# Attention values with transposed probabilities unscaled in float32 as the stationary operand, values with a column of ones moving, and scaling on the sums

## The chip, the cores and the metric

The kernel runs on one core of a Trainium2 chip. The metric is the device time of one execution in microseconds, from three runs. The profile is of one further execution, recorded by the hardware profiler.

## What is computed

The program is one layer of a decoder on 512 tokens of width 1024: a hybrid mixer, in which a recurrent branch (RG-LRU) and a sparse attention branch stand beside each other, and then a squared-ReLU MLP of width 4096. All inputs and outputs are float32. What matters here is the attention branch. Eight query heads share two groups of keys and values, and each head attends in three ways, which are gated and added:

```python
def one_block(i):
    ...
    p_c = jax.nn.softmax(sc, axis=-1) * (t >= CMP_LEN - 1)      # 31 compressed blocks
    o_c = jnp.einsum('bgrqc,bgcd->bgrqd', p_c, vc)
    ...
    p_s = jax.nn.softmax(ss.reshape(...), axis=-1)              # selected blocks
    o_s = jnp.einsum('bgrqnk,bgqnkd->bgrqd', p_s, v_sel)
    ...
    o_w = jnp.einsum('bgrqk,bgkd->bgrqd', jax.nn.softmax(sw, axis=-1), vwb)   # window
    return gb[0] * o_c + gb[1] * o_s + gb[2] * o_w
```

With 512 tokens all eight blocks are selected and the window covers all earlier tokens, so `selected` and `window` are both causal attention, over different keys and values. The attention output (512 tokens by 512) is normalised per token and multiplied with the lower half of `w_out`; the recurrent branch goes through the upper half.

## The kernel before, in words

Tokens stand in four tiles of 128. TensorE (PE) does matmuls in two ways. A float32 matrix that has been split into a high part `hi` and a rest `lo`, both of type float32r, is multiplied in three passes (`mm3`, line 986: hi·hi, hi·lo, lo·hi). Matrices that are left in plain float32 are multiplied as they are (`mm`, line 429). Splitting costs a copy (ACT or DVE) and a subtraction (DVE or POOL).

Work is written as streams, Python generators: `PR` does the projections, `AS` the attention's scores, `AV` its products with the values, `FA` the attention's end, `VW` the recurrent branch, `RS` the residual, `AD` the conditioning, `W` the loads and splits of weights, and later `TH` and `UF` (turning the normalised residual, first MLP slices), `UP`, `DA` and `DN` (MLP). They only record nodes: `Clocks.issue` and `Clocks.put` (lines 395 and 343) note each instruction with its operands and an assumed cost. `Clocks.flush` (line 237) then writes the instructions out in a list schedule: for each engine the ready node with the highest rank comes next, and the rank is the node's longest way to the end plus an offset from the table `AHEAD` (a number for every 20 steps of a stream). Where an operation may run on more than one engine (`choose`, `either`, `copy`), a letter of the table `PLACE` picks it: `a` ACT, `d` DVE, `p` POOL. So the order on every engine is fixed by these two tables and by the recorded costs, and the engines then run their instructions in that order.

Attention is cut into 16 units, each of one key group, one tile `i` of 128 queries and two heads (`UNITS`, line 46). For a unit and a head, `att_scores` (line 1416) multiplies queries and keys into a PSUM bank `s`. DVE adds the position bias and takes the row minimum `mx` on the way to a row of probabilities `p` in SBUF. ACT takes the exponential in place, one instruction for each of the three segments (compressed, selected, window), and its accumulator gives the segment's sum into `sm` (line 1464). Then `den`, the reciprocal of the sum times the gate's denominator, is made (lines 1465 to 1469), and each of the six segments is multiplied by its column of `den` in place (line 1473), on ACT, DVE or POOL.

`att_values` (line 1477) turns the scaled probabilities with PE, 128 by 128 at a time, four to a bank `tp` (line 1505), so that keys stand on partitions. It splits the bank into `hi` (copy, line 1508) and `lo` (subtraction, line 1509), both tiles `pt` from a ring of four. The values `V` and `VC` are the stationary operand, 128 wide: 64 columns of `hi` and 64 of `lo`, split once at lines 1085, 1086, 1124 and 1126. For each of the 2(i+1)+1 key blocks of a unit there are two matmuls of 256 columns (two heads by 128 queries), one with `hi` and one with `lo` (lines 1518 and 1520). All of them add into one bank `pv`. The upper 64 partitions (from the values' `lo`) are copied out by ACT into `oc` (line 1523) and added to the lower 64 by DVE (line 1525) into `att`. So `att` has features on partitions and queries along the row.

`att_finish` (line 1531) takes each finished tile of `att`: squares it (ACT), folds the squares by two additions, sums over partitions with a matmul against `ones`, and splits `att` into `hi` and `lo`, the stationary operands of the lower half of the output projection (line 1215, weights `o1..`). The upper half (weights `o0..`, line 1196) uses the recurrent branch. In the profile both halves are matmuls `f<-hi_o,h` and `f<-lo_o,h`. After them `residual` (line 1383) normalises, adds and normalises again per tile. `turn_h` (line 1567) turns the result and splits it into `h2` and `h2l`, and `up_first` (line 1596) begins the MLP with matmuls of 256 columns.

Of the kernel before, what the change touches and what calls it, by code (L numbers as in the profile page):

```python
# [32 lines left out]
RW = 528  # L33
G_LAST = 2
# [3 lines left out]
PART_BUFS = 4  # L38
SL = (0.0, 8.6, 11.4, 5.2)
# [67 lines left out]
    '': 'ad',  # L107
    'AS': 'ddd.p.a.ddapa..pdaddppapaa..paaadppd.d.pdadap.aa..ddd..pdadadd.dpa..a...a.d.adp.d.ddpa.add..paaa'
        'adpdpapaappd.aaa',
    'AV': '.ddaddd..d.dd...aadadaada..aaad..a...aaaaad.a.aaa..ada..',  # L110
    'AW': 'a.ad.aa.ddpp..dd',
    'DA': 'dd..d.dd.dddd.pa..dp..pdp.a..d...papd..dd.d.d.ddd..a.d.dap.a.d.pddpddd..pdd.d.appa.pa.pdddd.a..d'
        'pd.padp.pdd..d.ddda..a.p..adpapdddpd..pd..da.d.pddpa.dd.d.p.d..p...ddp...dd.ad.d',
    'DN': 'd..da.a.ada..d.d.pa.ad..a.ada.dd.da.ad.....dada...a....da.a...d..p.p....p.d.',
    'FA': 'd.....ppdd..',
    'RS': 'pdadddd.....',
    'TH': '..ddaa.p.a.ddad...dpadd..dpd.ad.',
    'UP': '.d.dddp..ppdd...pdp.dpp.d.ppdddd',
    'VW': '.ppdp.d.d.p..ppp.d.',
    'WS': 'a...a...a.ap.d..a.d.ap.d...p..adadapad..ddadd.apa.a.ada.ad.ad..dd.ddd.d.d.pd..d.ad.dp.dpadda.a..'  # L120
        '.d.dp...ad..a.dadda.dddad.dp.d.a..dd..a..dp.dp.d.ddd.pa.p..p.d..apda.dadddd.ddd.adddpddp..a.pddd'
        'dd.add.ddpd.dadp.d....p.d..ddadad..dd.dadpad.d..d.dda.da.....a.d.d..dd..ppada...ad..dd..a...a.a.'
        'd.ada.pda.ddpd.da..da.add......da.add.a.ad.dada.ddadddddadad.dada.',
    'XN': 'a.addd.dd.a.',
# [10 lines left out]
class Clocks:  # L135
# [370 lines left out]
    def zero(self, out):  # L506
        self.issue("pool", 0.1 + out.free_size() / 1100, [out], [], lambda: self.nc.gpsimd.memset(out, 0.0))
# [211 lines left out]
def block_kernel(tc, inp, out):  # L719
# [55 lines left out]
    def pt_tile(dt):  # L775
        return small(mp, "pt", 4, [P, 512], dt)
# [87 lines left out]
    for g in range(2):  # L864
        clk.zero(K2[g][64 - 64 * g:128 - 64 * g].bitcast(F32))
# [283 lines left out]
    def projections():  # L1149
        for g in range(2):  # L1150
            clk.zero(VC[g].bitcast(F32))
# [696 lines left out]
```

## Time and profile before

| | us |
|---|---|
| median of three runs | 644.36 (642.27 to 644.39) |
| the profiled execution | 643.96 |
| its span, from the first to the last instruction | 642.1 |
| busy: PE, DVE, ACT, POOL | 606.2, 550.3, 352.1, 179.9 |
| first and last transposes of probabilities `tp<-ident,p` | 115.5 and 268.4 |
| first and last exponentials of scores `p<-p,mx` | 101.9 and 258.3 |
| last `att<-pv,oc` | 271.7 |

A row of the profile's groups names the code line, the engine, the operation, then output and inputs by tile name, the shape, and the count after an x; behind the bar come busy time, the mean duration in ns, and the idle time of the engine in front of the group with what ended it. Busy time is the union of the records' durations. A matmul's record lasts longer than the distance to the next matmul, since matmuls are pipelined, so a PE that is busy for the whole of a stretch may still have free places in it. A row of the windows gives a stretch, its length, busy time with instruction count for PE, its weight loads (PEld), DVE, ACT and POOL, then the granted clock of PE, the share of the DMA engines and GB/s. A row of the timeline gives start, duration, engine, line, instruction and count.

### The profile page before, as it was taken

What the parts mean: (1) busy time and instruction counts of PE and PEld (TensorE: products, weight loads), DVE (VectorE), ACT (ScalarE), POOL (GpSimd) and SP (SyncE); (2) the same over time, 40 slices, a digit from 0 to 9 for tenths busy, and PEclk for the clock granted to TensorE, in tenths of its full rate; (3) what the DMA queues carried; (4) which work ended last, traced back from release to release, by engine and by line L of the source; (5) the groups of instructions that cost most, each with busy time, mean ns of one, the idle gap of its engine ahead of it and who ended that gap; (6) DMA issues with size and microseconds to landing.
All of it is one profiled execution on the core that took longest, in us unless ns stands there. A gap on an engine that the chain in (4) does not pass through costs nothing.

```text
span 642.1 us, 9070 instructions
## 1 busy us (share of the span) xinstructions
PE 606.2 (94%) x3060; PEld 499.8 (78%) x3060; DVE 550.3 (86%) x1097; ACT 352.1 (55%) x706; POOL 179.9 (28%) x175
## 2 busy tenths in 40 slices
PE   6899999997989999989999999999999999999992
PEld 6778788965776878868888878888878887888881
DVE  7988789989999999886898677575988779899988
ACT  6645436699999899786342332322332236645553
POOL 5010110424451013343212423653364212130022
PEclk9999999999999999997999999999999999999997
DMA  8968986430432202004764345343544425567613
GB/s 349 413 227 288 338 291 223 150 106 33 165 104 93 68 2 67 0 34 132 261 208 147 139 140 187 104 160 98 166 138 134 154 66 196 199 195 228 198 35 131
DMA packets 29431, 102.15 MB, mean 159 GB/s; under 512 B 3269, under 2 KB 3525, under 8 KB 29385
## 3 DMA queue, kind: packets, MB, share of 16 engines
q1 hardware_dynamic: 29240, 101.50, 46.1%
q8 instruction: 24, 0.39, 0.2%
q14 instruction: 23, 0.18, 0.1%
q10 hardware_dynamic: 144, 0.07, 0.0%
HBM read 99.47 MB, written 2.10 MB: 158 GB/s over the span
## 4 chain that ended last, share of the span: by engine, by line
PE 67%; DVE 15%; ACT 9%; DMA 6%; issue 2%; POOL 0%; DVEq 0%; ACTq 0%
PE f L434 36%; PE s L434 12%; PE pv L434 10%; PE tp L434 7%; DVE p L479 4%; ACT r L445 2%; DVE fT L479 2%; PE tp L438 2%; ACT p L445 2%; ACT h L445 2%; DVE pt L479 1%; ACT L445 1%; DMA p<-in_ada_a 1%; DVE r L479 1%; DVE h L479 1%
## 5 line engine op out<-in xcount | busy, mean ns | idle before, releaser
L434 PE MATMUL f<-h,lo_f 128*128 128x512 f32 x224 | 87.2, 389 | 0.0
L434 PE MATMUL f<-h,hi_f 128*128 128x512 f32 x224 | 87.2, 389 | 0.0
L434 PE MATMUL f<-h2l,hi_f 128*128 128x512 f32 x224 | 87.2, 389 | 0.0
L445 ACT ACTIVATE hi_f<-raw_f 128x1024 fp32r<-128x1024 f32 x25 | 26.3, 1067 | 45.2 <-PE f L434 26.4
L479 DVE TENSOR_TENSOR lo_f<-raw_f,hi_f 128x1024 fp32r<-128x1024 f32 x31 | 40.3, 1301 | 11.4 <-ACT hi_f L445 11.1
L434 PEld LDWEIGHTS f<-h,lo_f 128*128 128x128 f32 x224 | 42.1, 188 | 8.8
L434 PEld LDWEIGHTS f<-h2l,hi_f 128*128 128x128 f32 x224 | 42.1, 188 | 8.7
L434 PEld LDWEIGHTS f<-h,hi_f 128*128 128x128 f32 x224 | 42.1, 188 | 8.5
L445 ACT ACTIVATE p<-p,mx 128x32 f32<-128x32 f32 (+4 forms) x96 | 45.1, 473 | 1.8 <-DVE mx L479 1.5
L434 PE MATMUL f<-hi_o,h 128*128 128x512 f32 x128 | 44.2, 402 | 1.3 <-DVE h L479 1.3
L479 POOL TENSOR_TENSOR fT<-fT 128x512 f32<-128x512 f32 x19 | 28.3, 1492 | 54.3 <-ACT fT L445 54.3
L434 PE MATMUL pv<-pt,V 128*128 128x256 f32 x160 | 37.8, 328 | 0.9 <-ACT pt L445 0.7
L445 ACT ACTIVATE fT<-f 128x512 f32<-128x512 f32 x30 | 17.6, 588 | 37.5 <-PE f L434 37.5
L438 PE MATMUL tp<-ident,p 128*128 128x128 f32 x192 | 35.3, 274 | 0.8 <-DVE pt L479 0.7
L434 PE MATMUL s<-K,Q 128*128 128x288 f32 (+4 forms) x128 | 30.9, 332 | 5.1 <-DVE Q L479 3.4
L479 DVE TENSOR_TENSOR pt<-tp,pt 128x512 fp32r<-128x512 f32 (+1 forms) x56 | 32.9, 604 | 1.6 <-ACT pt L445 1.3
L438 PEld LDWEIGHTS tp<-ident,p 128*128 128x128 f32 x192 | 24.2, 140 | 8.3 <-DVE pt L479 2.6
L434 PEld LDWEIGHTS pv<-pt,V 128*128 128x128 f32 x160 | 26.2, 189 | 5.5 <-DVE pt L479 2.0
L445 ACT ACTIVATE fs<-fT 128x512 fp32r<-128x512 f32 x29 | 18.0, 626 | 18.8 <-PE s L434 9.7
L434 PEld LDWEIGHTS s<-K,Q 128*128 128x128 f32 x128 | 20.5, 188 | 9.9 <-DVE Q L479 3.4
L434 PEld LDWEIGHTS f<-hi_o,h 128*128 128x128 f32 x128 | 23.5, 188 | 5.6 <-DVE h L479 1.7
L434 PE MATMUL pv<-r,fs 128*128 128x512 f32 x96 | 25.8, 397 | 1.3 <-DVE r L479 1.3
(731 smaller groups left out, 1791.6 us busy)
## 6 DMA issues: line engine op xcount, KB each, us to landing
raw_f<-in_wf SPq DMA_DIRECT2D x32, 512.0 KB, 3.4
p<-in_ada_a SPq DMA_DIRECT2D x16, 512.0 KB, 8.4
ar<-in_ada_t SPq DMA_DIRECT2D x16, 512.0 KB, 5.2
ar<-in_ada_r SPq DMA_DIRECT2D x16, 512.0 KB, 4.0
r<-in_x SPq DMA_DIRECT2D x8, 512.0 KB, 5.8
raw_c<-in_wc SPq DMA_DIRECT2D x8, 512.0 KB, 4.9
raw_o<-in_wo SPq DMA_DIRECT2D x8, 512.0 KB, 3.5
raw_a<-in_wa SPq DMA_DIRECT2D x8, 384.0 KB, 7.9
```

The costliest lines, as they stand in the source:

```text
L434: lambda: self.nc.tensor.matmul(out, lhs, rhs, start=start, stop=stop))
L438: self.issue("pe", 0.109, [out], [src], lambda: self.nc.tensor.transpose(out, src, ident))
L445: return "act", cost, lambda: self.nc.scalar.activation(out, src, func, scale=scale, bias=bias, **kw), func
L479: return eng, cost, lambda: fn(out, *args, **kw), None
```

## The change

Probabilities are left unscaled. The exponential no longer writes its accumulator, `sm`, `den` and the six scalings of a unit go from `att_scores`, and `att_values` turns the unscaled probabilities. The turned block stays in float32 and is copied once. It is now the stationary operand, one block of one head at a time. The values are plain float32, 64 columns and a 65th of ones, and move. So a unit makes two matmuls of 65 columns for each key block (one for each head), and three sums for each head in one bank `pv`: three segments, two heads, 65 columns, where the 65th column holds the segment's sum of probabilities. `den` is made from these columns, one DVE multiplication scales all six blocks of 64 columns out of PSUM into `ov`, and two additions add the three segments into `att`, which now has queries on partitions. Groups of four transposes now hold up to four blocks of one head after the other, and the ring `pt` keeps its four buffers.

The values are copied once (ACT or DVE) and not split, and six fills on POOL write ones and zeros. `att_finish` squares `att` on ACT with the accumulator giving the row sum, turns `att` with four transposes, copies the bank to `hi` and subtracts for `lo`. It also waits for the event `yp` now. `AHEAD` and `PLACE` are other tables of numbers and letters, so the order and the engines of all streams change, the projections and the MLP among them.

```diff
-    'AV': [142.8, -8.6, 3.3, -42.5, -12.0, -9.0, 3.2, 261.5, 714.0, 604.8, -11.7, 349.8, 1400.4, 517.5, 179.8,
+    'AV': [507.0, -148.0, 17.4, 136.7, -64.4, 13.5, 178.9, 274.1, 572.1, 179.1, -46.5, 1110.1, 1841.6, 933.7,
...
-    V = [clk.lone(mp, [P, 4, P], F32R, name=f"V{t}") for t in range(NT)]
-    VC = [clk.lone(mp, [P, P], F32R, name=f"VC{g}") for g in range(2)]
+    V = [clk.lone(mp, [P, 4, VW_], F32, name=f"V{t}") for t in range(NT)]
+    VC = [clk.lone(mp, [P, 96], F32, name=f"VC{g}") for g in range(2)]
...
-            act(V[t][:, :, 0:64], src, AF.Copy)
-            dve("tensor_sub", V[t][:, :, 64:128], src, V[t][:, :, 0:64].bitcast(F32))
+            clk.copy(V[t][:, :, 0:64], src)
...
-                            act(seg, seg, AF.Exp, scale=-1.0, bias=col, accum_out=sm[:, si, e:e + 1])
-            den = small(mp, "den", 4, [P, 3, 2])
-            either("tensor_mul", den, sm, eg1[i][:, :, g, 2 * pair:2 * pair + 2])
-            dve("reciprocal", den, den)
...
-            for si, (a, b) in enumerate(segs):
-                for e in range(2):
-                    seg = tiles[e][:, a - base:b - base]
-                    clk.copy(seg, seg, den[:, si, e:e + 1])
+                            act(seg, seg, AF.Exp, scale=-1.0, bias=col)
...
-                    hi, lo = pt_tile(F32R)[:, :w], pt_tile(F32R)[:, :w]
-                    clk.copy(hi, tp[:, :w])
-                    dve("tensor_sub", lo, tp[:, :w], hi.bitcast(F32))
+                    pt = pt_tile(F32)[:, :w]
+                    clk.copy(pt, tp[:, :w])
...
-                        mm(po, v, hi[:, sl], done == 0, False)
-                        done += 1
-                        mm(po, v, lo[:, sl], False, done == n)
-            o = att[i][:, tok(2 * g + pair)]
-            oc = small(mp, "oc", 2, [64, 256])
-            act(oc, po[64:128, :], AF.Copy)
-            for e in range(2):
-                dve("tensor_add", o[64 * e:64 * e + 64], po[0:64, tok(e)], oc[:, tok(e)])
+                    for k, (e, _, v, si, first, last) in enumerate(sub):
+                        mm(po[:, si, e, :], pt[:, tok(k)], v, first, last)
+            den = small(mp, "den", 4, [P, 3, 2])
+            dve("tensor_mul", den, po[:, :, :, 64], eg1[i][:, :, g, 2 * pair:2 * pair + 2])
+            dve("reciprocal", den, den)
+            if i == 0:
+                dve("tensor_scalar", den[:, 0, :], den[:, 0, :], cmask, None, op0=ALU.mult)
+            ov = small(mp, "ov", 2, [P, 3, 2, 64])
+            dve("tensor_mul", ov, po[:, :, :, 0:64], den.unsqueeze(3).to_broadcast([P, 3, 2, 64]))
+            o = att[i][:, tok(2 * g + pair)].rearrange("p (e d) -> p e d", e=2)
+            either("tensor_add", ov[:, 0], ov[:, 0], ov[:, 1])
+            either("tensor_add", o, ov[:, 0], ov[:, 2])
...
-            yield after(f"pv{t}", lambda: clk.ready(att[t]))
-            sq = cmt[:, 0:512]
-            act(sq, att[t], AF.Square)
-            hi, lo = h_tile(), h_tile()
-            act(hi, att[t], AF.Copy)
-            either("tensor_sub", lo, att[t], hi.bitcast(F32))
-            for w in (256, 128):
-                either("tensor_add", sq[:, 0:w], sq[:, 0:w], sq[:, w:2 * w])
...
-            mm(ps[:, 0:1], sq[:, 0:P], ones[:, 0:1], True, True)
+            yield after(f"pv{t}", after("yp", lambda: max(clk.ready(att[t]), bank_free("tp"))))
             r = scol()
-            dve("tensor_copy", r, ps[:, 0:1])
+            act(junk[:, 0:512], att[t], AF.Square, accum_out=r)
...
+            for k in range(4):
+                turn(ps[:, tok(k)], att[t][:, tok(k)], ident)
+            hi, lo = h_tile(), h_tile()
+            clk.copy(hi, ps)
+            dve("tensor_sub", lo, ps, hi.bitcast(F32))
```

Two places show what the tables and the new steps do to the order. The first is PE where attention ends, before the change: the last products with the values of the last unit (`pv`), then a transpose for the MLP (`tp<-ident,r`) and the output projection (`f`).

```order
L434 MATMUL pv_733<-pt_738,V_122 128x256
L434 MATMUL pv_733<-pt_739,V_122 128x256
L434 MATMUL pv_733<-pt_738,V_123 128x256
L434 MATMUL pv_733<-pt_739,V_123 128x256
L434 MATMUL pv_733<-pt_743,VC_124 128x256
L434 MATMUL pv_733<-pt_744,VC_124 128x256
L438 MATMUL tp_773<-ident,r_282_502 128x128
L434 MATMUL f_745<-lo_o_662,h_650 128x512
```

The same place on PE after the change: the last products have 65 columns and one block of one head each.

```order
L439 MATMUL tp_657<-ident,p_644 128x128 x2
L435 MATMUL pv_652<-V_120,pt_656 128x65
L435 MATMUL pv_652<-V_121,pt_656 128x65
L435 MATMUL pv_652<-V_122,pt_656 128x65
L435 MATMUL pv_652<-V_123,pt_658 128x65
L435 MATMUL pv_652<-VC_124,pt_658 128x65
L435 MATMUL f_661<-hi_o_530,h_513 128x512
L435 MATMUL f_692<-hi_o_582,h_517 128x512
```

Behind the last product with the values there are 43 matmuls of the output projection before the change and 97 after it; the transposes for the MLP, which began there before, come later.

The second place is DVE in the last unit before the change: subtractions for `lo`, a scaling by `den`, the residual's rows `r`, and the two additions into `att`.

```order
L479 TENSOR_SCALAR p_704<-p_704,den_715 128x32
L479 TENSOR_TENSOR pt_736<-tp_734,pt_735 128x512
L479 SCALAR_TENSOR_TENSOR r_282_502<-f_740,stat,r_282_502 128x512
L479 CAST pt_743<-tp_742 128x256
L479 TENSOR_TENSOR pt_739<-tp_737,pt_738 128x512
L479 TENSOR_TENSOR pt_744<-tp_742,pt_743 128x256
L479 TENSOR_TENSOR r_282_502<-r_282_502,h_469 128x512
L479 TENSOR_TENSOR r_282_502<-r_282_502,h_470 128x512
L479 TENSOR_TENSOR att_129<-pv_733,oc_747 64x128 x2
```

The same place on DVE after the change: one copy of a turned bank, `den`, the scaling out of PSUM, the additions, and splits of the output projection's weights between them.

```order
L480 COPY pt_658<-tp_657 128x256
L480 TENSOR_TENSOR den_659<-pv_652,eg_133 128x6
L480 RECIPROCAL den_659<-den_659 128x6
L480 TENSOR_TENSOR ov_660<-pv_652,den_659 128x384
L480 SCALAR_TENSOR_TENSOR lo_o_694<-raw_o_532,vecs,hi_o_693 128x512
L480 TENSOR_TENSOR ov_660<-ov_660 128x128
L480 SCALAR_TENSOR_TENSOR lo_o_694<-raw_o_532,vecs,hi_o_693 128x512
L480 TENSOR_TENSOR att_129<-ov_660 128x128
L480 SCALAR_TENSOR_TENSOR r_318_547<-f_692,stat,r_318_547 128x512
L480 CAST h_666<-tp_665 128x512
L480 TENSOR_TENSOR h_667<-tp_665,h_666 128x512
```

The three subtractions and the scaling are gone from this stretch. The rows `r` of the residual, which stood between the unit's steps, come behind them.

More of the change, by code (lines that the diff above doesn't have):

```diff
@@ L33 @@
 RW = 528
+VW_ = 80
 G_LAST = 2
@@ L38 @@
 PART_BUFS = 4
+PT_BUFS = 4
 SL = (0.0, 8.6, 11.4, 5.2)
@@ L504, in copy, with fill @@
         self.choose([out], [src] + cols, "ad", *ways)
-    def zero(self, out):
-        self.issue("pool", 0.1 + out.free_size() / 1100, [out], [], lambda: self.nc.gpsimd.memset(out, 0.0))
+    def fill(self, out, value=0.0):
+        self.issue("pool", 0.1 + out.free_size() / 1100, [out], [], lambda: self.nc.gpsimd.memset(out, value))
     def dve(self, what, out, *args, **kw):
@@ L1031, in block_kernel @@
     blk = blkt.rearrange("p a b -> p (a b)")[:, :2048].rearrange("p (v l c) -> p v l c", v=2, l=16)
-    clk.zero(blkt.rearrange("p a b -> p (a b)")[:, :2048])
+    clk.fill(blkt.rearrange("p a b -> p (a b)")[:, :2048])
     cmt = clk.lone(mp, [P, 768], F32, name="cmt")
@@ L1124, in compress_out @@
             act(VC[g][0:32, 0:64], pc2[:32, 64 * g:64 * g + 64], AF.Copy)
-        for g in range(2):
-            dve("tensor_sub", VC[g][0:32, 64:128], pc2[:32, 64 * g:64 * g + 64], VC[g][0:32, 0:64].bitcast(F32))
         events.add("vc")
@@ L1150, in projections @@
         for g in range(2):
-            clk.zero(VC[g].bitcast(F32))
+            clk.fill(VC[g])
+            clk.fill(VC[g][0:32, 64:65], 1.0)
+        for t in range(NT):
+            clk.fill(V[t][:, :, 64:65], 1.0)
         load(cmt[:, 0:384], inp["w2"])
         rnn["xpad"] = r8()
-        clk.zero(rnn["xpad"][:, :, 0:3])
+        clk.fill(rnn["xpad"][:, :, 0:3])
         for item in ORDER:
@@ L1239, in ada_sum @@
         acc = accT
-        clk.zero(acc)
+        clk.fill(acc)
         load(acc[0:1, :], inp["ada_b"][0:1, part * D + n * 512:part * D + n * 512 + 512])
@@ L1463, in att_scores @@
                             seg = pt[:, a - base:b - base]
-                            act(seg, seg, AF.Exp, scale=-1.0, bias=col, accum_out=sm[:, si, e:e + 1])
-            den = small(mp, "den", 4, [P, 3, 2])
-            either("tensor_mul", den, sm, eg1[i][:, :, g, 2 * pair:2 * pair + 2])
-            dve("reciprocal", den, den)
-            if i == 0:
-                dve("tensor_scalar", den[:, 0, :], den[:, 0, :], cmask, None, op0=ALU.mult)
-            for si, (a, b) in enumerate(segs):
-                for e in range(2):
-                    seg = tiles[e][:, a - base:b - base]
-                    clk.copy(seg, seg, den[:, si, e:e + 1])
+                            act(seg, seg, AF.Exp, scale=-1.0, bias=col)
             scored[u] = tiles
@@ L1481, in att_values @@
         for u, (g, i, pair) in enumerate(units):
-            blocks = [(b * P, V[i - b][:, g, :]) for b in range(i + 1)]
-            blocks += [((i + 1) * P + 32 + b * P, V[b][:, 2 + g, :]) for b in range(i + 1)]
-            blocks.append(((i + 1) * P, VC[g]))
-            n, done = len(blocks), 0
-            groups = [blocks[k:k + 2] for k in range(0, n, 2)]
+            blocks = [(b * P, V[i - b][:, g, :65], 1) for b in range(i + 1)]
+            blocks += [((i + 1) * P + 32 + b * P, V[b][:, 2 + g, :65], 2) for b in range(i + 1)]
+            blocks.append(((i + 1) * P, VC[g][:, :65], 0))
+            ends = [(k == 0 or blocks[k - 1][2] != si, k + 1 == len(blocks) or blocks[k + 1][2] != si)
+                    for k, (_, _, si) in enumerate(blocks)]
+            blocks = [(e, *b, *z) for e in range(2) for b, z in zip(blocks, ends)]
+            groups = [blocks[k:k + 4] for k in range(0, len(blocks), 4)]
             turned = []
@@ L1492, in can_turn @@
                         return INF
-                    return max([bank_free("tp")] + [clk.ready(scored[u][e][:, b[0]:b[0] + P])
-                                                    for b in groups[0] for e in range(2)])
+                    return max([bank_free("tp")] + [clk.ready(scored[u][b[0]][:, b[1]:b[1] + P]) for b in groups[0]])
                 def can_times():
-                    return max(clk.ready(turned[0][0], turned[0][1]), bank_free("pv") if po is None else 0.0)
+                    return max(clk.ready(turned[0][0]), bank_free("pv") if po is None else 0.0)
                 if groups and len(turned) < 2:
@@ L1502, in att_values @@
                     tp = bank("tp")
-                    for k, (c0, _) in enumerate(sub):
-                        for e in range(2):
-                            turn(tp[:, tok(2 * k + e)], scored[u][e][:, c0:c0 + P], ident)
-                    w = 256 * len(sub)
-                    hi, lo = pt_tile(F32R)[:, :w], pt_tile(F32R)[:, :w]
-                    clk.copy(hi, tp[:, :w])
-                    dve("tensor_sub", lo, tp[:, :w], hi.bitcast(F32))
-                    turned.append((hi, lo, sub))
+                    for k, (e, c0, *_) in enumerate(sub):
+                        turn(tp[:, tok(k)], scored[u][e][:, c0:c0 + P], ident)
+                    w = P * len(sub)
+                    pt = pt_tile(F32)[:, :w]
+                    clk.copy(pt, tp[:, :w])
+                    turned.append((pt, sub))
                 else:
@@ L1513, in att_values @@
                     if po is None:
-                        po = bank("pv")[:, :256]
-                    hi, lo, sub = turned.pop(0)
-                    for k, (_, v) in enumerate(sub):
-                        sl = slice(k * 256, k * 256 + 256)
-                        mm(po, v, hi[:, sl], done == 0, False)
-                        done += 1
-                        mm(po, v, lo[:, sl], False, done == n)
-            o = att[i][:, tok(2 * g + pair)]
-            oc = small(mp, "oc", 2, [64, 256])
-            act(oc, po[64:128, :], AF.Copy)
-            for e in range(2):
-                dve("tensor_add", o[64 * e:64 * e + 64], po[0:64, tok(e)], oc[:, tok(e)])
+                        po = bank("pv")[:, :390].rearrange("p (s e d) -> p s e d", s=3, e=2)
+                    pt, sub = turned.pop(0)
+                    for k, (e, _, v, si, first, last) in enumerate(sub):
[10 more added lines that the diff above has]
+            either("tensor_add", o, ov[:, 0], ov[:, 2])
             events.add(f"u{u}")
```

45 lines of the change are left out of this document (21 added, 24 removed), and 64 rows, old and new, of the table AHEAD.

## The prediction

> **What bounds the kernel now.** I read the page's first two lines, then the windows by stage, then one stretch instruction by instruction.
>
> ```profile
> span 642.1 us, 9070 instructions
> PE 606.2 (94%) x3060; PEld 499.8 (78%) x3060; DVE 550.3 (86%) x1097; ACT 352.1 (55%) x706; POOL 179.9 (28%) x175
> 40.00:100.00 60.00, 59.60 (x330) 50.03 (x328) 50.71 (x78) 24.56 (x39) 6.15 (x4) 1.00 0.81 277
> 100.00:320.00 220.00, 206.71 (x1201) 171.77 (x1200) 201.45 (x547) 182.88 (x438) 64.90 (x73) 0.98 0.29 100
> 200.00:280.00 80.00, 79.04 (x480) 66.80 (x479) 75.14 (x211) 68.78 (x169) 16.28 (x27) 1.00 0.13 40
> 320.00:480.00 160.00, 159.63 (x711) 131.15 (x709) 121.61 (x189) 48.48 (x77) 61.55 (x51) 1.00 0.46 150
> ```
>
> PE is busy 94% of the span. The change lies between 100 and 320 us: attention, the recurrent branch and the handover to the MLP. There DVE is busy 201.5 of 220 us and ACT 182.9, and PE, by its records, 206.7. Before and behind it PE has almost no free time, though DVE is busy there too.
>
> A matmul's record is longer than the distance to the next matmul, so PE has more room than 220 - 206.7 = 13.3 us. The distances come from runs of equal matmuls.
>
> ```profile
> 413.91 33.56 PE f L434 x148
> 184.73 0.63 PE L434 MATMUL pv<-pt,V 128*128 128x256 f32 x4
> 246.82 0.60 PE L438 MATMUL tp<-ident,p 128*128 128x128 f32 x4
> 72.06 3.79 PE L434 MATMUL s<-r,raw_c 128*128 128x64 f32 x32 [0.22 <-DMA raw_c<-in_wc]
> 132.48 1.02 PE L434 MATMUL s<-r,p 128*128 128x512 f32 x2
> ```
>
> 512 columns in float32r: 33.56/148 = 0.227 us each. 256 columns: a last record of about 0.28, so (0.63 - 0.28)/3 = 0.117. A transpose: (0.60 - 0.27)/3 = 0.11. Plain float32 with 64 columns: (3.79 - 0.28)/31 = 0.113 for a record. Now one stretch by these distances:
>
> ```profile
> L434 PE MATMUL f<-h,hi_g 128*128 128x512 f32 x22 | 7.5, 400 | 0.5 <-ACT r L445 0.5
> L434 PE MATMUL f<-h,hi_q 128*128 128x512 f32 x15 | 4.8, 395 | 0.0
> L434 PE MATMUL f<-h,lo_g 128*128 128x512 f32 x10 | 3.9, 394 | 0.0
> L434 PE MATMUL f<-h,lo_q 128*128 128x512 f32 x8 | 3.2, 406 | 0.0
> L434 PE MATMUL pv<-pt,V 128*128 128x256 f32 x8 | 1.8, 305 | 0.0
> L434 PE MATMUL s<-K,Q 128*128 128x288 f32 (+1 forms) x6 | 1.6, 339 | 3.4 <-DVE Q L479 3.4
> L438 PE MATMUL tp<-ident,p 128*128 128x128 f32 x5 | 1.0, 272 | 0.0
> L434 PE MATMUL pv<-pt,VC 128*128 128x256 f32 x3 | 0.9, 307 | 0.0
> ```
>
> These are PE's groups from 140 to 160 us: 55 x 0.227 + 11 x 0.117 + 6 x 0.13 (288 columns) + 5 x 0.11 = 15.1 us of work in 20. The free 5 us are mostly waits for DVE and ACT. The same reckoning over the 1201 records from 100 to 320 gives 192 us of work, so **28 us are free**. For 200 to 280 it gives 75.8 of 80 (5% free), for 40 to 100 57.8 of 60 (4%), for 320 to 480 158.8 of 160 (1%). The free time is largest from 140 to 200 (12.8 us) and from 280 to 300 (7.2 us).
>
> Part of the second is a slower clock:
>
> ```profile
> 285.00:290.00 5.00, 3.08 (x18) 2.24 (x18) 3.55 (x7) 5.00 (x9) 2.73 (x4) 0.98 0.00 0
> 290.00:295.00 5.00, 4.29 (x20) 4.30 (x21) 5.00 (x6) 2.95 (x5) 1.74 (x2) 0.50 0.53 162
> 295.00:300.00 5.00, 5.00 (x38) 5.00 (x38) 1.61 (x3) 1.67 (x2) 0.13 (x1) 0.84 0.76 252
> ```
>
> PE was busy 3.1 of 5 us, and then the granted clock stood at 0.50 for five us and at 0.84 for the next: 2.5 + 0.8 = 3.3 us lost. [...]
>
> **The change part by part.** PE first, since it gets more to do.
>
> ```profile
> L434 PE MATMUL pv<-pt,V 128*128 128x256 f32 x160 | 37.8, 328 | 0.9 <-ACT pt L445 0.7
> L434 PE MATMUL s<-r,raw_c 128*128 128x64 f32 x128 | 15.1, 275 | 0.2 <-DMA raw_c<-in_wc 0.2
> ```
>
> Before, the products with the values are 160 matmuls with `V` and 32 with `VC`: 192 x 0.117 = 22.5 us. After, they are 192 plain float32 matmuls of 65 columns. The nearest row is the compression's float32 product of 64 columns: the code (line 1101) issues 64 of these and the trace has 128 records, so one counts as two. 192 x 2 x 0.113 = 43.4 us. The ends: if cost followed the width, a record would be 65/512 of the 512-column float32 record, whose distance is 1.02 - 0.59 = 0.43 us, so 0.055 and 21 us in all; but 64 columns show 0.113, twice that. I take 43.4, since one column more is all that differs. [...]
>
> The 16 transposes of `att` add 16 x 0.11 = 1.8, the four sums against `ones` go (under 1 us). **PE gains about 22 us of work**: 192 becomes 214 in the stage.
>
> The other engines lose work.
>
> ```profile
> L479 DVE TENSOR_TENSOR pt<-tp,pt 128x512 fp32r<-128x512 f32 (+1 forms) x56 | 32.9, 604 | 1.6 <-ACT pt L445 1.3
> L479 DVE TENSOR_SCALAR p<-p,den 128x32 f32<-128x32 f32 (+4 forms) x37 | 14.7, 427 | 0.1
> L479 DVE TENSOR_TENSOR att<-pv,oc 64x128 f32<-64x128 f32 x32 | 9.0, 281 | 2.2 <-ACT oc L445 1.5
> L445 ACT ACTIVATE p<-p,den 128x32 f32<-128x32 f32 (+4 forms) x43 | 19.8, 507 | 0.8 <-DVE den L479 0.8
> L445 ACT ACTIVATION_READ_ACCUMULATOR p<-p,mx 128x1 f32 x96 | 18.3, 191 | 0.0
> L445 ACT ACTIVATE oc<-pv x16: 381/381/383, 121.5 to 270.8; 64x256 f32<-64x256 f32 x16
> L479 DVE TENSOR_TENSOR pt<-tp,pt x56: 402/676/692, 117.8 to 269.7; 128x512 fp32r<-128x512 f32 x40, 128x256 fp32r<-128x256 f32 x16
> L445 ACT ACT_TABLE_LOAD x14 | 18.0, 1283 | 1.4 <-PEq L1837 1.2
> L479 POOL TENSOR_SCALAR p<-p,den 128x32 f32<-128x32 f32 (+4 forms) x16 | 14.2, 892 | 42.1 <-DVE den L479 31.6 <-DVE att L479 6.2 <-PE f L434 3.8
> ```
>
> DVE loses the subtractions (32.9), its scalings (14.7) and the additions into `att` (9.0), 56.6 us. It gains 16 scalings out of PSUM of 384 columns, between the 0.40 of 256 columns and the 0.68 of 512, so 0.54 each, 8.6; by the order 22 additions of 128 columns at 0.28, 6.2; and some five more copies of turned banks at about 0.6, 3. **DVE: about -39 us.** ACT loses scalings (19.8), accumulator reads (18.3) and the `oc` copies (16 x 0.38 = 6.1), 44.2; the order shows four more table loads at 1.28, 5.1. **ACT: about -39 us.** POOL loses 14.2 and gains ten short additions. In the stage DVE would then stand at 162 of 220, ACT at 144: neither can be the bound. What is late next is PE.
>
> None of this counts by itself: a step saved on DVE or ACT is worth only the PE time that it frees. A turned bank also waits for one copy instead of a copy and a subtraction, which takes 0.68 us out of the way from transposes to products. A new wait: `att` must be turned and split behind the last unit, where the order puts 97 output matmuls (97 x 0.227 = 22 us) on PE, against 43 before, so PE has work through that step. The order of loads on SP moves with the tables; DMA is busy only 29% of this stage, so I put it at nothing. A late weight would cost about what the MLP's first weights (`hi_f`, `lo_f`) cost in PE's groups from 280 to 300, 0.5 + 0.7 us:
>
> ```profile
> L434 PE MATMUL pv<-h2l,hi_f 128*128 128x256 f32 x16 | 5.8, 361 | 1.5 <-DVE h2l L479 1.4
> L434 PE MATMUL pv<-h,lo_f 128*128 128x256 f32 x16 | 5.7, 358 | 0.7 <-DVE lo_f L479 0.7
> L434 PE MATMUL pv<-h,hi_f 128*128 128x256 f32 x16 | 5.5, 346 | 0.5 <-ACT hi_f L445 0.5
> ```
>
> The fills on POOL come early, and POOL is busy for only 28% of the span: nothing.
>
> **The sum.** The stage takes 214/(1 - u), where u is PE's free share. u = 12.8% now. With DVE and ACT at some 75% and 65%, it should lie between the 1% of the MLP and the 5% of 200 to 280, where DVE is busy 94%; I take 3%, a little under the 4% of 40 to 100. 214/0.97 = 220.6, or +0.6 us. At the program's end
>
> ```profile
> 636.43 2.74 DVE L479 SCALAR_TENSOR_TENSOR fT<-fT,stat,r 128x512 f32<-128x512 f32 x4
> ```
>
> four multiplications follow the last reciprocal, and the order leaves three: -0.7 us. So 643.96 + 0.6 - 0.7 = **643.9 us**, no change: 22 us of matmul work fill 21 us of holes. The profiled execution lies 0.4 under the median of 644.36. A measurement can tell about 0.5%, 3.2 us; with the tail that is u between 1.6% and 4.4%.
>
> **The rivals.**
>
> *The holes close altogether.* DVE and ACT were what PE waited for (the groups above name `Q` on DVE), 39 us of relief is far more than the 28 free us, and the halved clock goes with the holes. With the MLP's 1%, 214/0.992 = 215.7, or -4.3; with the tail 639.0, and 637.3 with no hole at all. For it: the order has output matmuls to fill in with. Against it: 200 to 280 keeps 5% though nothing there is short of work. The Trainium skill (Perfetto Trace Analysis, Identifying the Most-Contended Engine) would have one judge by the occupancy of the vector engine and not by PE's busy share, and so relieve DVE first; the windows agree up to the point where PE is full.
>
> *The handover keeps its hole.* Between the last output matmul and the MLP's first, PE waits for a chain: residual, square, scale, turn, `h2l` (1.5 us before the MLP's first matmuls, in the rows above). That is latency, not load, and the change does not shorten it. If PE falls idle there again and the clock is halved, the 7.2 free us of 280 to 300 stay. With 3% of the other 200 us, 6, that makes 13.2 free us: 214 + 13.2 = 227.2, or +7.2, 650.5 with the tail. It decides from 9.9 free us in the stage on (4.4%). If holes of the recurrent branch (140 to 200) stay too, it is 655 or more.
>
> *The products cost by width.* If a 65-column float32 record takes 0.055, PE gains 22 - 22.4, nothing; the stage is 192/0.97 = 198, -22, and the time 621. The 128 records of `raw_c` speak plainly against it.
>
> **How the numbers follow.** No change 0.40, holes closed 0.31, handover or branch slower 0.27, cost by width 0.02. So faster 0.33, same 0.40, slower 0.27. The forecast is the likeliest case. Its own range is 640.8 to 647.2. The range for 8 in 10 reaches to the middle of both other cases: 635 (holes closed, and a us or two from the new order elsewhere) to 653 (half-way between 650.5 and 655).
>
> **What would show it.** The products `pv` should have 384 records 0.113 apart; at half that the third rival holds. PE's work from 100 to 320 should rise by 22 us and its free time fall from 28 to about 7; `pt<-tp,pt`, `oc` and the accumulator reads of `p` are gone; DVE should fall to about 160 and ACT to about 145 busy us of the 220. A granted clock under 1 behind the last attention tile, with `h2l` as the releaser, would show the handover's hole. A stage in which DVE or ACT still runs above 90% would prove the step wrong that takes them off the bound.

## The result and the profile after

The changed kernel takes 650.0 us (median of 20 runs, 647.2 to 653.9) and the kernel before, on the same chip, 646.5 (20 runs, 642.1 to 654.5). The ratio is 1.0059, with a 95% interval of 1.0034 to 1.0083: **slower by 0.6%**, some 4 us, where 643.9 and no change were forecast. The profiled execution took 648.15 us with a span of 646.4, against 643.96 and 642.1: 4.3 us more span.

The changed kernel's page and windows, to set against the prediction's first fence:

```profile
span 646.4 us, 9158 instructions
PE 616.5 (95%) x3260; PEld 518.5 (80%) x3260; DVE 520.0 (80%) x993; ACT 326.0 (50%) x559; POOL 176.8 (27%) x174
```
```profile
40.00:100.00 60.00, 57.45 (x310) 48.11 (x309) 49.44 (x77) 21.61 (x35) 6.96 (x3) 1.00 0.73 262
100.00:320.00 220.00, 211.94 (x1372) 183.95 (x1372) 159.13 (x449) 150.14 (x278) 54.81 (x58) 1.00 0.29 97
200.00:280.00 80.00, 80.00 (x525) 69.93 (x525) 51.37 (x155) 39.74 (x76) 11.24 (x20) 1.00 0.12 40
320.00:480.00 160.00, 158.67 (x720) 130.74 (x718) 129.43 (x180) 51.22 (x84) 66.33 (x54) 1.00 0.46 155
```

The relief came as worked out: from 100 to 320 us DVE is busy 159 us (201 before) and ACT 150 (183). From 200 to 280 PE is now busy throughout by its records; by the distances between them 1.4 of the 80 us are free (2%), where it was 5%. The chain that ended last, from the page, by engine (before, PE 67%, DVE 15%, ACT 9%):

```profile
PE 85%; DVE 6%; DMA 4%; ACT 3%; POOL 1%; issue 1%; SPq 0%; DVEq 0%; POOLq 0%; ACTq 0%
```

PE's groups of the attention (100 to 285 us), the scores' group in the same window before the change, and the timeline of one run of products:

```profile
L435 PE MATMUL pv<-V,pt 128*128 128x65 f32 x320 | 44.7, 267 | 0.0
L439 PE MATMUL tp<-ident,p 128*128 128x128 f32 x192 | 34.2, 274 | 0.0
L435 PE MATMUL s<-K,Q 128*128 128x256 f32 (+4 forms) x128 | 32.2, 346 | 1.2 <-DVE den L480 0.7 <-DVE mx L480 0.4
L435 PE MATMUL pv<-VC,pt 128*128 128x65 f32 x64 | 11.7, 264 | 0.0
```
```profile
L434 PE MATMUL s<-K,Q 128*128 128x288 f32 (+4 forms) x128 | 30.9, 332 | 5.1 <-DVE Q L479 3.4 <-DVE mx L479 1.2
```
```profile
241.71 2.12 PE L435 MATMUL pv<-V,pt 128*128 128x65 f32 x18
```

There are 384 records in 70 runs, (2.12 - 0.27)/17 = 0.109 us apart in the one shown and 0.103 on average. Within a run most are 0.112 apart, and the first of a run ends only some 0.06 behind the matmul ahead of it. The scores' wait, 5.1 us before, is 1.2; the transposes and products wait for nothing.

Then the handover. The five-us windows behind the last output products, and PE's groups from 280 to 320:

```profile
285.00:290.00 5.00, 4.42 (x22) 3.12 (x22) 5.00 (x7) 3.36 (x7) 2.23 (x3) 1.00 0.33 105
290.00:295.00 5.00, 3.85 (x25) 2.86 (x23) 5.00 (x9) 5.00 (x12) 3.18 (x2) 1.00 0.64 210
295.00:300.00 5.00, 2.23 (x16) 2.02 (x17) 4.79 (x10) 4.01 (x8) 1.50 (x1) 1.00 0.01 3
300.00:305.00 5.00, 3.31 (x28) 3.11 (x28) 3.83 (x6) 2.16 (x4) 2.65 (x4) 1.00 0.32 105
```
```profile
L435 PE MATMUL pv<-h2l,hi_f 128*128 128x256 f32 x30 | 8.8, 292 | 2.4 <-DVE h2l L480 2.4
L435 PE MATMUL pv<-h,lo_f 128*128 128x256 f32 x29 | 8.4, 289 | 1.2 <-DVE lo_f L480 1.2
...
L439 PE MATMUL tp<-ident,r 128*128 128x128 f32 x32 | 5.1, 281 | 2.6 <-ACT r L446 1.7 <-ACT h L446 0.4 <-DVE h L480 0.3
```

The hole is there as before, with `h2l`, `lo_f` and `r` as releasers, but it is made of other parts. Between the last output product and the last transpose PE sat idle for 3.2 us before, and most of the rest was the halved clock that the prediction shows from 290 us on. Now the clock stays at 1.00, and PE sits idle for 5.9 us. The transposes, for one, hardly waited before (PE's group from 280 to 300 us):

```profile
L438 PE MATMUL tp<-ident,r 128*128 128x128 f32 x15 | 2.4, 280 | 0.2 <-ACT h L445 0.2
```

The length of a pause alone doesn't tell when the clock is halved. The longest pause here is 1.98 us, in front of an `h2l` product, and the clock stays at 1.00. Before the change it was halved at 290 us, though no pause from 200 us on had been longer than 1.38 us, and it stayed at 1.00 from 140 to 200 us, in spite of a pause of 3.08 us there. These are the two matmuls behind those pauses (the pause is the figure in brackets):

```profile
151.09 0.53 PE L434 MATMUL s<-K,Q 128*128 128x288 f32 x2 [3.08 <-DVE Q L479]
287.67 0.38 PE L434 MATMUL pv<-h2l,hi_f 128*128 128x256 f32 x1 [1.38 <-DVE h2l L479]
```

The Trainium skill (TensorE: Matmul & The Clock Gate, The HAM clock gate) has the clock halved after an idle window of some 3.4 us. The trace before the change doesn't agree, since the clock was halved there without such a pause; what sets it off is left open.

To put the time in its place I cut the span at three events that every kernel of this study has: the first score product, the last output product, and the last transpose of the turned residual. PE's free time is reckoned as in the prediction, from the distance between records less what the matmul itself takes; pauses under 0.04 us count as work, and what a halved clock costs counts as free.

| us | first score at | to the last output product (free) | to the last transpose (free) | to the end |
|---|---|---|---|---|
| before | 100.8 | 181.7 (18.3) | 21.7 (7.8) | 337.9 |
| changed | 102.7 | 188.2 (7.6) | 21.0 (7.5) | 334.5 |
| difference | +1.9 | +6.5 (-10.7) | -0.7 (-0.3) | -3.4 |

The attention is 6.5 us longer: its holes closed by 10.7, and PE's work grew by 17. The handover takes as long as it did, with more idle time and without the halved clock. Behind it the new order gives 3.4 us back. The 1.9 in front is within scatter: eight kernels with this same order of the first 100 us have their first score at 102.3 to 108.6, the late ones with a clock of 0.94 from 40 to 100 us.

### The profile page after: what moved, and what is told of

The parts are those of the page before. It is cut to its first block, busy times and chain, and to the rows that moved or that the text cites. A ratio compares the mean times of both kernels' runs of the same rounds, so it can differ in the third digit from the quotient of the medians.

```text
span 646.4 us, 9158 instructions
## 1 busy us (share of the span) xinstructions
PE 616.5 (95%) x3260; PEld 518.5 (80%) x3260; DVE 520.0 (80%) x993; ACT 326.0 (50%) x559; POOL 176.8 (27%) x174
## 4 chain that ended last, share of the span: by engine, by line
PE 85%; DVE 6%; DMA 4%; ACT 3%; POOL 1%; issue 1%; SPq 0%; DVEq 0%; POOLq 0%; ACTq 0%
PE f L435 41%; PE s L435 16%; PE pv L435 15%; PE tp L435 8%; PE tp L439 4%; DMA ar<-in_ada_r 2%; ACT h L446 1%; DMA raw_a<-in_wa 1%; DVE fT L480 1%; POOL stat L480 1%; DMA raw_v<-in_wv 1%; POOL lo_x L480 1%; DMA raw_c<-in_wc 1%; DVE p L480 0%; DVE accT L480 0%
## 5 line engine op out<-in xcount | busy, mean ns | idle before, releaser
L480 DVE TENSOR_TENSOR lo_f<-raw_f,hi_f 128x1024 fp32r<-128x1024 f32 x30 | 38.5, 1288 | 13.6 <-ACT hi_f L446 13.1
L446 ACT ACTIVATE p<-p,mx 128x32 f32<-128x32 f32 (+4 forms) x96 | 40.8, 473 | 13.6 <-DVE mx L480 13.4
L435 PE MATMUL pv<-V,pt 128*128 128x65 f32 x320 | 44.7, 267 | 0.0
L435 PEld LDWEIGHTS pv<-V,pt 128*128 128x128 f32 x320 | 42.2, 191 | 2.0 <-ACT pt L446 0.7
L480 POOL TENSOR_TENSOR fT<-fT 128x512 f32<-128x512 f32 x19 | 27.0, 1425 | 55.0 <-ACT fT L446 55.0
L446 ACT ACTIVATE fs<-ft 128x256 fp32r<-128x256 f32 x36 | 14.9, 414 | 45.2 <-DVE ft L480 24.2
L435 PE MATMUL s<-K,Q 128*128 128x256 f32 (+4 forms) x128 | 32.2, 346 | 1.2 <-DVE den L480 0.7
L480 DVE COPY pt<-tp 128x512 f32<-128x512 f32 (+1 forms) x26 | 15.4, 596 | 13.9 <-PE tp L439 13.8
L480 DVE SCALAR_TENSOR_TENSOR accT<-ar,sil,accT 128x512 f32<-128x512 f32 x32 | 25.1, 786 | 1.4 <-DMA ar<-in_ada_r 1.3
```

Of the source, the lines that this page charges most:

```text
L435: lambda: self.nc.tensor.matmul(out, lhs, rhs, start=start, stop=stop))
L446: return "act", cost, lambda: self.nc.scalar.activation(out, src, func, scale=scale, bias=bias, **kw), func
L480: return eng, cost, lambda: fn(out, *args, **kw), None
```

## The experiments

The theory at the start: PE is the bound now, and the 17 to 20 us that it got cost more than the holes that closed. Rivals: the attention is paced by the chains over DVE and ACT, whatever PE does; the new tables are at fault; the handover's hole has a cause of its own.

**e1: PE's added work taken away, order held.**

```diff
-    V = [clk.lone(mp, [P, 4, VW_], F32, name=f"V{t}") for t in range(NT)]
+    V = [clk.lone(mp, [P, 4, VW_], F32R, name=f"V{t}") for t in range(NT)]
...
-                    pt = pt_tile(F32)[:, :w]
+                    pt = pt_tile(F32R)[:, :w]
```

> The changed kernel with the products of probabilities and values as one float32r matmul each (66 columns moving, probabilities and values rounded to float32r) in place of plain float32, in the same order on every engine. What is computed is less precise; the place of every instruction is kept. It takes 192 of the 384 records of pv away, 192 x 0.109 = 21 us of TensorE work between 120 and 270 us, and nothing from any other engine. Theory PE (TensorE is the bound of the attention now, and the added 20 us of matmul work are what ate the gain): 648 - 15 to 21 = 627 to 633 us in the profile. Rival chain (the attention is bound by chains of scores, exponentials and copies on the other engines, and TensorE's records only fill what is free): less than 8 us gained, 640 to 648, and TensorE's gaps between 120 and 270 grow by more than 13 us.

648.5 us, ratio 1.0037 (1.0008 to 1.0067): next to nothing. PE's groups from 100 to 285 us, and two windows:

```profile
L440 PE MATMUL tp<-ident,p 128*128 128x128 f32 x192 | 34.7, 286 | 2.1 <-ACT pt L447 1.5 <-DVE pt L481 0.5
L436 PE MATMUL s<-K,Q 128*128 128x256 f32 (+4 forms) x128 | 32.8, 349 | 4.9 <-DVE mx L481 1.8 <-DVE den L481 1.4 <-DVE Q L481 1.3
L436 PE MATMUL pv<-V,pt 128*128 128x66 f32 x160 | 29.2, 274 | 2.1 <-DVE pt L481 1.2 <-ACT pt L447 0.8
```
```profile
205.00:210.00 5.00, 4.50 (x28) 3.89 (x29) 2.38 (x8) 1.99 (x4) 3.54 (x5) 0.87 0.00 0
210.00:215.00 5.00, 5.00 (x14) 3.98 (x14) 1.50 (x5) 0.38 (x1) 1.11 (x2) 0.50 0.01 3
```

The waits for `mx`, `pt` and `Q` are back, and so is a halved clock, which costs some 3 us in these two windows (0.13 and 0.50 of five us each). From the first score to the last output product it is 183.9 us, 26.0 of them free: the free time grew by 18.4 us, and only 4.3 are gained. As it stood, my theory fell here, and the rival of the chains seemed right.

**e2 and e14: DVE's load put back, order held.** In e2 DVE adds two SBUF tables behind each of the 56 copies; in e14 it subtracts the copy from the bank, as before the change, into a tile that nobody reads.

Each edit is issued with the copy and is not known to the planner; the first line is e2's, the second e14's:

```diff
+                    nc.vector.tensor_add(spare, tabf, tabf)
...
+                    nc.vector.tensor_sub(spare[:, :w], tp[:, :w], pt)
```

> The changed kernel with the relief of VectorE taken back: behind each of the 56 copies of a turned bank VectorE adds two 512-column tables into a spare tile that nobody reads, 56 x 0.68 = 38 us, in the order of the changed kernel. No wait is added for any other engine but for the time that VectorE is taken. Theory PE (the relief closed the attention's holes, 18.5 us before and 6.8 after between 100 and 280): VectorE at about 197 of 220 busy reopens them, 8 to 14 us slower, 656 to 662 us. Rival (the holes closed because of the new order and the shorter waits for a bank, not because of VectorE's load): less than 4 us slower.

> The changed kernel with one part of the removed work put back: behind the copy of each of the 56 turned banks VectorE subtracts the copy from the bank into a spare tile that nobody reads, 56 x 0.60 = 33 us, and the bank is held until then, as it was before the change; the matmuls don't wait for it. Theory load (VectorE has room in the changed kernel; what is put back fills it first): VectorE at about 192 of 220, 6 to 14 us slower. Rival (e2 was slow by 31 us because any long operation of VectorE between copy and score stands in the way of an order fitted without it): 20 us slower or more.

e2: 679.8 us, ratio 1.0509 (1.0463 to 1.0556). e14: 670.7, 1.0367 (1.0322 to 1.0413). PE's groups of e14 from 100 to 305 us:

```profile
L435 PE MATMUL pv<-V,pt 128*128 128x65 f32 x320 | 44.9, 267 | 0.8 <-DVE pt L480 0.8
L439 PE MATMUL tp<-ident,p 128*128 128x128 f32 x192 | 35.2, 279 | 6.0 <-DVE spare L1501 4.8 <-DVE den L480 1.0
L435 PE MATMUL s<-K,Q 128*128 128x256 f32 (+4 forms) x128 | 33.4, 352 | 6.4 <-DVE mx L480 5.1 <-DVE den L480 0.9
```

Against the changed kernel's 650.0, the subtractions of e14, 34 us on DVE, cost 21, at the rival's edge; the additions of e2, 43 us, cost 30, which is above both of its expectations. DVE is far from full in e14 (178 of 220 us), but the bank waits for the subtraction and the scores for `mx` behind it. Why e2 costs a little more per us was not separated.

**e3 and e4: the tables exchanged.** One entry of the many, in e3:

```diff
-    'FA': [858.0, -32.6],
+    'FA': [7.9, 538.3],
```

> The changed kernel with the tables of order and engines of the kernel before (a pick that names an engine which the operation no longer has falls back to the usual one). Rival order (the arithmetic is worth something and the new tables lose it, in the handover and at 60 to 80 us): the time falls to 640 us or less. Theory PE (the arithmetic itself is worth nothing; a table fitted to other work is at best as good): 648 to 665 us.

> The kernel before with the tables of the changed kernel, with the same fallback. Rival order: the new tables carry their loss along, 3 to 5 us in the handover and at 60 to 80 us, and little else: 648 to 652 us. Theory PE: the tables fit the arithmetic that they were made for, so this is slower by an amount that the two places don't explain: above 652 us.

675.8 us (1.0451, 1.0402 to 1.0501), above both expectations, and 704.8 (1.0902, 1.0854 to 1.0950), as theory PE had it. An order is worth 30 to 60 us to the arithmetic it was made for, several times the effect in question. So e1, e2 and e14 tell what happens when work is taken from or put into an order that was made for other work: little is won, much is lost. What the work itself costs needs an order made for it.

**e5, e6, e7: each arithmetic with an order fitted to it.** The edit is in `AHEAD` and `PLACE`, here one entry of e5; e7 has also e1's edit.

```diff
-    'FA': [858.0, -32.6],
+    'FA': [9344.2065, 15644.8756],
```

> The changed kernel's arithmetic with new tables of order and engines, fitted to it by further search (as many steps as for the two kernels below). Theory fit (a static order takes up whatever the engines' work leaves; the first table of the changed kernel was only fitted less well, and that made it slower): 2 to 6 us less than the changed kernel's 650. Theory PE (TensorE's work is in the way and a better order can't help): within 2 us of 650.

> The arithmetic of the kernel before, with tables fitted by the same search. Theory fit with TensorE's price in full: it gains as much as the changed kernel does or more, 638 to 643, and stays 4 to 10 us below it, since it has 20 us less for TensorE to do. Rival (with equal fitting the new arithmetic, which takes 39 us off VectorE and 39 off ScalarE, is the faster): at or above the refitted changed kernel.

> The products of the values as one float32r matmul each, as in the first experiment (less precise, 21 us less for TensorE), but the planner now knows their cost, and the tables are fitted by the same search. Theory PE (the 21 us of matmul work are the price of the change, and the first experiment gave nothing only because its order was made for a TensorE that is busy at those places): 12 to 21 us below the refitted changed kernel. Rival chain (the attention is paced by VectorE and ScalarE whatever TensorE does): less than 6 us below it.

e5: 662.3 us, 1.0196 (1.0141 to 1.0252). e6: 652.0, 1.0081 (1.0053 to 1.0109). e7: 647.4, 1.0010 (0.9976 to 1.0043). None of these orders is a good one, and that they would gain was a miss: e5 and e6 lose to the tables they replace. Among themselves they are nearer to comparable, and there the order of the three is that of PE's work: single products, then the kernel before, then the changed one.

**e9, e12, e13: the same, with only the middle fitted anew** and the first 100 us and the MLP left as they are, so that losses elsewhere don't blur it. One entry of e13:

```diff
-    'FA': [858.0, -32.6],
+    'FA': [3738.1971, -4809.5335],
```

> The products of the values as one float32r matmul each, as in the first experiment, its order fitted anew only for the steps between some 100 and 300 us; the first 100 us and the MLP keep the entries of the changed kernel's tables. Theory PE (the 21 us of matmul work are the price of the change once the order is fitted to them): 13 to 20 us below the changed kernel's 650, faster than the kernel before by 1.5 to 2.5%. Rival chain: less than 6 us below the changed kernel.

> The kernel before, its order fitted anew only for the steps between some 100 and 300 us, as in e9. Theory PE: at or below the kernel before (0 to 6 us less), and 4 to 10 us below the changed kernel that is refitted in the same way. Rival (the new arithmetic is the faster one under equal fitting): at or above the refitted changed kernel.

> The changed kernel, its order fitted anew only for the steps between some 100 and 300 us. Theory PE: TensorE is nearly full from the first score to the last output product (7.6 us free of 188), so an order can give at most those 7.6 us and what the handover leaves: 646 to 652, still above the kernel before. Rival: 643 or less, the first table was at fault.

e9: 639.3 us, 0.9853 (0.9815 to 0.9891). e12: 643.0, 0.9945 (0.9921 to 0.9969). e13: 655.3, 1.0128 (1.0082 to 1.0175). So e9 is 10.7 us below the changed kernel, where 13 or more were expected, and e13 lies above its 646 to 652. The windows from 100 to 320 us, e9, e12 and e13 in turn:

```profile
100.00:320.00 220.00, 208.90 (x1268) 178.20 (x1267) 173.21 (x466) 154.42 (x287) 51.57 (x58) 0.99 0.34 112
```
```profile
100.00:320.00 220.00, 211.24 (x1252) 179.50 (x1251) 203.60 (x552) 177.30 (x431) 83.65 (x88) 0.98 0.31 103
```
```profile
100.00:320.00 220.00, 212.59 (x1350) 184.70 (x1349) 159.92 (x445) 150.06 (x276) 53.17 (x59) 0.98 0.27 91
```

DVE is busy 204 of 220 us in e12 and 160 in e13, and e12 is the faster. By the cuts of the table above:

| us from the first score to the last transpose | first tables | all fitted | middle fitted |
|---|---|---|---|
| before | 203.4 | 201.8 (e6) | 195.1 (e12) |
| changed | 209.2 | 209.4 (e5) | 212.9 (e13) |
| single products | 205.7 (e1, not fitted) | 193.3 (e7) | 193.8 (e9) |

Two things are read from the columns. Some 20 us of PE work, the difference of the last two rows, are worth 16 and 19 us as soon as the order is made for it, and 3.5 when it isn't. The changed kernel's two fitted orders are worse than its first; against the first one's 209.2 it is still 16 and 15. And with PE's work no larger than before, the relief of 39 us each on DVE and ACT is worth 1 to 9 us, the difference of the first and last rows. By the ratios of all executions, without any cut, PE's work is worth 1.9 and 2.8% (some 12 and 18 us) and the relief 0.7 and 0.9% (5 and 6). So the change pays 12 to 19 for PE and gets a few us for the relief; in three pairs of tables it is the slower one three times. Theory PE stands in this form. That a better table exists for the changed kernel isn't excluded: two more searches found none, but a search that ends above its start says little. The sizes are rough: one arithmetic's two fitted orders differ by 0.5 to 6.7 us here, each of the six fitted profiles has 3 to 17 us of halved clock in the stretch, and the one of e5 took 655.2 us, 7 under its median. So 1 to 9 for the relief says little more than that it is far below the price of the matmuls.

**e8, e10, e11, e15: the handover.** e8 takes the reciprocal roots off GpSimd:

```diff
+            nc.scalar.activation(ss, ss, AF.Sqrt)
+            nc.vector.reciprocal(ss, ss)
...
+                  lambda: nc.vector.tensor_scalar(ss, ss, 1.0 / width, EPS, op0=ALU.mult, op1=ALU.add))
```

e10 leaves out the second norm (what lies between the two marks isn't issued, and `plain` takes the place of the scaling):

```diff
+            clk.blank = {"Square", "stat"}
             act(junk, x2, AF.Square, accum_out=ss2)
             rstd_of(ss2, D)
+            clk.blank = set()
...
+            plain = [clk.act_way(y, x2, AF.Copy, scale=0.5), clk.elem_way("dve", "tensor_scalar", y, x2, 0.5, None, op0=ALU.mult), clk.elem_way("pool", "tensor_scalar", y, x2, 0.5, None, op0=ALU.mult)]
```

e11 leaves out the float32 copies; e15 has both edits:

```diff
-                    clk.choose([o], [i, a, b], "ad", clk.act_way(o, i, AF.Identity, scale=a, bias=b),
-                               clk.elem_way("dve", "tensor_scalar", o, i, a, b, op0=ALU.mult, op1=ALU.add))
+                    clk.choose([o], [i, a, b], "ad", *[(*w_[:2], lambda: None, w_[3]) for w_ in ways])
...
-                    either("tensor_sub", h2l[kk_][:, ts2], hf[:, k * 256:k * 256 + 256], h2[kk_][:, ts2].bitcast(F32))
+                    clk.choose([o], [i, j], "d", *[(*clk.elem_way(e_, "tensor_sub", o, i, j)[:2], clk.elem_way(e_, "tensor_sub", o, j, j)[2], None) for e_ in ("dve", "pool")])
```

> The changed kernel with the reciprocal roots of the residual's norms taken from GpSimd (two short instructions, of which the first waited for up to 4.12 us while VectorE ran one long operation after the other) to VectorE, ScalarE and VectorE again, all else in the same order. Theory chain (the handover's hole is the chain of the residual, and GpSimd's waits of 3.9 and 3.0 us are part of it): the wait of the transposes for ScalarE's r, 1.9 us, goes, and 1.5 to 4 us are gained. Rival (the handover waits for ScalarE's affine copies and the late split of the weights; the norm of the later tiles is hidden behind them): within 1 us, one table load of 1.28 us more on ScalarE.

> The changed kernel without the second norm of the residual: its squares on ScalarE, its sums' read-out and its two steps on GpSimd are not issued, and the row is scaled by one half instead of by the reciprocal root (left out: the root of the mean square ahead of the MLP). All else in the same order. Some 2.3 us shorter per tile on the chain from the output product to the transposes. Theory chain (TensorE's 7.5 free us between the last output product and the last transpose are the latency of the residual's chain): 2 to 4 us less. Rival affine (they are ScalarE's fifteen affine copies in a row and the late split of the MLP's first weights): within 1 us.

> The changed kernel without the float32 copies hf of the turned rows (16 affine copies, 15 of them on ScalarE); the low part h2l of the MLP's input is the difference of its high part with itself, so zero (left out: the low part). The matmuls with it and the subtractions stay, all in the same order. Theory chain: within 1.5 us of the changed kernel. Rival affine: 2 to 4 us less, with TensorE's wait for h2l at about 295 us (2.2 us) gone.

> The changed kernel without the second norm (as in e10) and without the float32 copies hf (as in e11) at once; the row is scaled by one half, and the low part is zero. If the two links lie one behind the other, their gains add: 1 to 2 us more than in e10. If they lie side by side, each hidden by the other (theory parallel chains), TensorE's free time between the last output product and the last transpose falls from 7.5 to 4 us or less, and 3 to 5 us are gained. If the late split of the first weights (lo_f, 1.2 us) decides, that wait stays and the gain is under 2 us.

e8: 650.5 us, 1.0068 (1.0036 to 1.0100). e10: 648.0, 1.0022 (0.9994 to 1.0049). e11: 649.5, 1.0056 (1.0023 to 1.0088). e15: 648.2, 1.0030 (0.9996 to 1.0065). PE's groups from 280 to 320 us, first of e8, then of e15:

```profile
L435 PE MATMUL f<-hi_o,h 128*128 128x512 f32 x22 | 7.8, 408 | 0.8 <-DVE stat L866 0.8
L439 PE MATMUL tp<-ident,r 128*128 128x128 f32 x32 | 5.1, 281 | 2.3 <-ACT r L446 0.8 <-DVE r L480 0.7 <-ACT h L446 0.4
```

```profile
L439 PE MATMUL pv<-h2l,hi_f 128*128 128x256 f32 x30 | 8.9, 296 | 2.6 <-DVE h2l L484 2.2 <-POOL h2l L484 0.4
...
L439 PE MATMUL pv<-h,lo_f 128*128 128x256 f32 x29 | 8.4, 289 | 1.2 <-DVE lo_f L484 1.2
...
L443 PE MATMUL tp<-ident,r 128*128 128x128 f32 x32 | 4.9, 275 | 1.0 <-ACT r L450 0.8 <-DVE r L484 0.2
```

In e8 the wait for ACT's `r` falls from 1.7 to 0.8 us, and one for DVE's `stat` of 0.8 takes its place. The handover's free time is 7.5 (e8), 6.6 (e10), 6.3 (e11) and 5.4 us (e15), against 7.5. By these four profiles, one of each kernel, the two links' gains add (0.9 + 1.2 = 2.1), so they lie one behind the other rather than side by side; in e15 the waits for `h2l` and `lo_f` stay, 2.6 and 1.2 us. Of the 2.8 us that e15 is ahead at the last transpose, counted from the first score, 2.4 are lost again in the MLP. In all 17 kernels this stretch has 5.4 to 11.5 free us. No single link that I took out holds it; what would close it is left open.

## Why the prediction was wrong

Its likeliest case was no change; what came is nearest to the second rival, that the handover keeps its hole. Step by step:

- **PE's added work** was forecast at 22 us, with 0.113 for a record of 65 columns: the kind of cost (a record each, twice a product, not by width) is right, the size was too large. The records came 0.103 apart: within a run the prediction's figure holds (0.112), but the first of each of the 70 runs takes only some 0.06. The old ones came 0.120 apart rather than 0.117, so 384 x 0.103 - 192 x 0.120 = 16.5; with 1.8 for the transposes of `att` and 0.9 for the sums that went it is 17.4. By itself this error would have made the kernel faster than forecast.
- **DVE and ACT** at 160 and 145 busy us of 220: 159 and 150. Right. That a stage with one of them above 90% would prove them the bound was too strict a test: from 140 to 200 ACT is still busy 56.7 of 60 us, hardly less than the 57.7 before, and yet PE has only 2.6 us free, where the prediction found 12.8. The window after and before, and ACT's costliest group in it after:

```profile
140.00:200.00 60.00, 59.23 (x375) 51.50 (x374) 47.65 (x141) 56.68 (x94) 24.35 (x20) 1.00 0.25 89
```
```profile
140.00:200.00 60.00, 52.40 (x269) 41.35 (x268) 57.83 (x157) 57.74 (x133) 27.07 (x25) 1.00 0.26 92
```
```profile
L446 ACT ACT_TABLE_LOAD x13 | 16.7, 1283 | 0.2
```

- **PE's free time was to "fall from 28 to about 7": this step failed.** "I take 3%" was put on the whole stage. By the cuts it was 26.1 free us before and 15.1 after, 7% of the stretch and not 3%. The attention alone came near it (7.6 of 188.2, 4.0%). The handover's 7.5 of 21.0 us did not shrink (7.8 before), and I had seen why: "That is latency, not load, and the change does not shorten it". I wrote this under a rival and left it out of the sum. That the size stayed the same is itself part chance, since the idle time grew from 3.2 to 5.9 us while the halved clock went; why the waits grew was not separated. The 15.1 lie above the 9.9 from which that rival decides. Its price of 650.5 met the 650.0 of the runs, though in part by chance: PE's work was smaller than it took, and the halved clock that it allowed for didn't come.
- **Behind the stage** only the tail was in the sum, -0.7; measured from the last matmul to the end -0.8 (12.2 to 11.35). The rest of the 3.4 us given back goes with smaller holes in the MLP under the new order (some 5 us free before, 2.0 now), which the sum had at nothing. In front, the order of loads that I put "at nothing" makes the compression's products wait for a load, 0.2 us before (the 128 records in the prediction) and now, from 40 to 100 us:

```profile
L435 PE MATMUL s<-r,raw_c 128*128 128x64 f32 x114 | 13.7, 272 | 1.6 <-DMA raw_c<-in_wc 1.6
```

- **The holes close altogether** failed on the handover as well, and not where I had argued against it: from 200 to 280 the free 5% did fall, to 2%. **Cost by width** is refuted by the 0.103.

Behind the failed step is a looser one. I reckoned that relief turns into PE time one for one until PE is full. The fitted kernels show that 39 us each off DVE and ACT buy 1 to 9 us, in a stage where DVE was busy 92% of the time, while some 20 us of PE's work are paid at 12 to 19.

## What to carry to other kernels

In this stage TensorE was busy 94% of the time and VectorE 92%. In such a place price TensorE's added work nearly in full, and relief of the other engine only by the holes it closes, hole by hole: a hole that is a chain's latency at a handover stays in the sum. An experiment that takes work out of a static order or puts it in, and keeps the order, measures the order more than the work; fit an order to each before comparing, and trust a fit that ends above its start only for rough sizes. The fastest kernels of the study come from that: the kernel before with its middle fitted anew (e12, 0.9945, 0.9921 to 0.9969), and, with less precise products, e9 (0.9853, 0.9815 to 0.9891).

## What the runs showed of the hardware

Two short steps on GpSimd lie in the handover's chain. In the changed kernel's timeline one of them, a single column, spans 4.12 us instead of its usual 0.19, while DVE ran one long operation after the other (the columns are start and duration):

```profile
288.51 4.12 POOL L480 TENSOR_SCALAR stat<-stat 128x1 f32<-128x1 f32 x1 [1.97 <-ACT junk L446]
292.72 0.55 POOL L480 TENSOR_TENSOR stat<-stat,nhalf 128x1 f32<-128x1 f32 x1
```

The Trainium skill (GPSIMD Engine Reference, Specifications) has GpSimd's SBUF interfaces shared with VectorE, in contention with operations of two SBUF inputs; DVE's stretch from 288.4 to 292.6 is of such operations, which agrees, though it is one span, and no run takes those operations away. Taking the steps off GpSimd (e8) nevertheless gained nothing: others were as late.
